# Weight rows of 8 KB, and turned tiles moved within SBUF in 16 pieces, in a two-layer encoder kernel

## The chip, the core and the metric

The kernel runs on one core of a Trainium2 chip, in one launch. The metric is device time in microseconds (us). The times before are 2138.24 us (median of three runs, 2136.27 to 2146.2). One further execution was profiled: it took 2142.62 us, and the span of its instructions is 2140.9 us. Every number of a profile is from that execution.

## What is computed

256 rows of 2048 floats go through two layers. All data are float32.

```python
# layer A                                       D = 2048, H = 16 heads of 128, FF = 8192
u = rms_norm(h, g);  q, k, v, fz = split(u @ a_w_in)          # (D, 3D + H)
q, k = rms_norm per head;  o = causal softmax attention with a forget bias
h = h + o @ a_w_out                                            # (D, D)
h = h + relu(rms_norm(h, g) @ mlp_w1[0]) ** 2 @ mlp_w2[0]      # (D, FF), (FF, D)
# shared keys and values, once, from h
k, v = split(rms_norm(h, g) @ kv_w)                            # (D, 2D)
# layer B
q = rms_norm(rms_norm(h, g) @ b_w_q);  o = chunked attention with a bias by distance
h = h + o @ b_w_out
h = h + relu(rms_norm(h, g) @ mlp_w1[1]) ** 2 @ mlp_w2[1]
```

## The kernel before

**Units.** Weights are consumed in units of 128 x 1024 floats, 512 KB each, 972 in all. For each unit, ScalarE (ACT) copies it, rounded, into `hi` and VectorE (DVE) writes the rest, `lo = raw - hi` (`issue`, L253 and L254). TensorE (PE) then makes three passes over it, hi by hi, hi by lo of the activations, and lo by hi (`passes`, L538, L540, L542). There are three `hi` and three `lo` buffers (pool `wsp`), and `fetch` keeps two units split ahead of the one being multiplied (`AHEAD`). A product unit is 12 matmuls (two k tiles, two row blocks, three passes).

**Pairs.** The two MLPs and the query projection use a Strassen-like scheme that needs seven block products where eight stand, on the first half of the k range of two neighbouring output panels. Such a `Pair` has seven forms, f0 to f6, each in two units of 6 matmuls, and eight product units a4 to a7 and b4 to b7. The forms' weights come from four blocks "11", "12", "21", "22" of 128 x 2048: `bring` (L276) loads a block into SBUF, `add` (L283) adds another block to it by an accumulating DMA of GpSimd (POOL), `make` (L290) adds two of them on DVE, and form 4 adds once more on DVE (L260). A chunk of an MLP is two pairs of w1 and two of w2; each MLP has four chunks.

**The written order.** `keep_order` fixes the order of every engine but POOL to that of the program text. `plan_mlp` deals the units of a stage by the strings in `ORDER` ("f0" is a form with both of its units, "a4" a product unit of the pair, "r" one left over from the pair before). `BEHIND` and `OPENING` say how many units after a form `bring`, `add` and `make` are written. Everything else (statistics, attention, the turning of tiles) is queued by `add_fill` and written one slot after each product unit or second form unit (`run_fill`). `HIDDEN`, `LONG` and `SHORT` hold, per output panel, the slots of the steps of a turned tile.

**Turned tiles.** A result of 256 x 512 has to be transposed before it can be an operand. DVE transposes its 32 x 32 blocks into `z`, 128 x 1024 (`blocks32`, L397). Then `carry` (from L408) brings the blocks to their partitions by way of HBM: `rows` writes `z` to a buffer `turn` in one DMA (L413), and `columns` reads it back in four DMAs of 32 partitions (L419). The four wait for the write. ACT uses the result in `take` (L896, the hidden layer), `split_turned` (L373, the normed residual) or `scale_q` (L662). `sums` (L355 to L364) then makes the form operands `Sh` and `S` of the first two panels: four DVE instructions, two ACT instructions on their result, two DVE instructions on that. 60 tiles are turned so, and 32 smaller ones in attention.

**Loading.** All DMAs but the accumulating ones are issued by SyncE (SP), in written order. `load` (L240) fetches one unit into one of six `raw` buffers; `fetch` keeps five loaded ahead (`EARLY`). In the built program every DMA of SP also waits for the eighth DMA that SP issued before it: eight are in flight at most.

Of the kernel before, what the change touches and what calls it, by code (L numbers as in the profile page):

```python
# [32 lines left out]
LONG = ((0, 0, 1, 3, 6, 7, 8, 8), (0, 0, 0, 1, 5, 5, 6, 6), (0, 0, 0, 0, 5, 6), (0, 0, 0, 2, 6, 6))  # L33
SHORT = ((3, 0, 1, 3, 5, 5, 7, 8), (6, 1, 2, 5, 10, 10, 14, 14), (3, 0, 3, 4, 8, 10), (0, 0, 0, 2, 5, 5))
REL = 384
ORDER = {
# [9 lines left out]
}  # L46
BEHIND = {
    (0, 0): [(0, 1, "make", 0)],
    (0, 1): [(0, 1, "make", 1), (1, 1, "add", "T1", 1)],
    (1, 0): [(3, 0, "bring", "12", 0)],  # L50
    (1, 1): [(2, 0, "bring", "12", 1)],
    (3, 0): [(2, 0, "bring", "11", 0)],
    (3, 1): [(2, 0, "bring", "11", 1)],
    (2, 0): [(1, 1, "add", "T1", 0)],
    (6, 1): [(5, 0, "add", "T3", 1)],
    (5, 0): [(2, 0, "add", "T3", 0)],
}
OPENING = (
    (20, "bring", "12", 0),
    (8, "bring", "12", 1),  # L60
    (8, "add", "T3", 0),
    (4, "add", "T3", 1),
    (7, "bring", "11", 0),
    (5, "bring", "11", 1),
# [17 lines left out]
def trunk(ctx: ExitStack, tc: tile.TileContext, xT, xr, gs, hg, bf, wgate, w_in, w_oa, f1a, s1a, f2a, s2a,  # L82
          w_kv, fqb, sqb, w_ob, f1b, s1b, f2b, s2b, rel, out):
# [9 lines left out]
    wraw = pool("wraw", 6)  # L93
# [42 lines left out]
    def queue(src, m):  # L136
        u = [src[i] for i in range(m)]
        n = KT // UA
        u[: 2 * n] = [u[i + q * n] for i in range(n) for q in range(2)]
        units.extend(u)  # L140
# [6 lines left out]
    class Tail:  # L147

        def __init__(self, src, first):
            self.left = [4]  # L150
            self.src = [[None] * (KT // UA - 4) + [src[first + u] for u in range(4)]]

    class Pair:

        def __init__(self, big, src, stage, n):
            self.big, self.src, self.stage, self.n = big, src, stage, n
            self.left = [6, 5]
            self.ps, self.t, self.done, self.prev, self.next = None, {}, set(), None, None

        def did(self, *names):  # L160
            return all((i, s) in self.done for i in names for s in range(2))

        def items(self, names):
            for i in names.split():
                if i[0] == "f":
                    for s in range(2):
# [4 lines left out]
    def pairs_of(f, s, c, stage):  # L171
        n = D // UN
        out = []
        for q in range(f.shape[0] // 4 // c[1]):
            i = c[0] * (f.shape[0] // 4 // c[1]) + q
            big = dict(zip(("11", "12", "21", "22"), (f[4 * i + j] for j in range(4))))
            src = [[None] * 4 + [s[8 * i + 4 * j + u] for u in range(4)] for j in range(2)]
            out.append(Pair(big, src, stage, q))
        return out

    def plan_mlp(w1, w2, wq, tail):
        pairs = []
        for c in range(NCH):
            pairs += pairs_of(*w1, (c, NCH), ("w1", c))
            pairs += pairs_of(*w2, (c, NCH), ("w2", c))
        if wq:
            pairs += pairs_of(*wq, (0, 1), ("q", 0))
        plan, rest = [], [Item(tail, 0, u) for u in range(KT // UA - 4, KT // UA)]
        for i, p in enumerate(pairs):
            own = list(p.items("a4 a5 a6 a7 b4 b5 b6 b7"))  # L190
            for j in ORDER["first" if not i else p.stage[0] + str(p.n) + ("+" if p.stage == ("w2", NCH - 1) else "")].split():
                if j == "r":
# [4 lines left out]
                else:  # L197
                    k = next(k for k in own if (k.kind, k.u) == ("ab".index(j[0]), int(j[1])))
# [5 lines left out]
        for p in pairs:  # L204
            g = lambda i, s=1: at[id(p), "f", i, s]
            assert g(0) < g(2, 0) and g(1) < g(2) < g(3, 0) and g(2) < g(5, 0) and g(3) < g(6, 0) and g(0) < g(4, 0)
            assert all(at[id(p), q, u, 0] > g((2, 3)[q]) for q in range(2) for u in range(4, 8))
# [5 lines left out]
    for i in range(w_in.shape[0]):  # L213
        units.append(w_in[i])
    n_out = w_oa.shape[0] - 4
    queue(w_oa, n_out)
    tail_a = Tail(w_oa, n_out)
    plan_a = plan_mlp((f1a, s1a), (f2a, s2a), (fqb, sqb), tail_a)
    for i in range(w_kv.shape[0]):
        units.append(w_kv[i])  # L220
    queue(w_ob, n_out)
    tail_b = Tail(w_ob, n_out)
    plan_b = plan_mlp((f1b, s1b), (f2b, s2b), None, tail_b)
# [4 lines left out]
    def load(parts=1):  # L228
        src, item = units.popleft(), None
        if isinstance(src, Item):  # L230
            item = src
            if item.u not in (4, 6):
                raws.append((item, None, ()))
                return
            src = item.pair.big[FORMS[item.u]][:, item.s * UN : (item.s + 1) * UN]
        raw = wraw.tile([P, UN], F32, name="raw")
        n = UN // parts
        cuts = [slice(i * n, (i + 1) * n) for i in range(parts)]
        for c in cuts:
            SY.dma_start(raw[:, c], src[:, c])  # L240
        raws.append((item, raw, cuts))

    def issue(parts=1):
        if not raws:
            load(parts)
        item, raw, cuts = raws.popleft()
        if not cuts:
            assert (FORMS[item.u], item.s) in item.pair.done
            raw, cuts = item.pair.t[FORMS[item.u]][:, item.s * UN : (item.s + 1) * UN], [slice(0, UN)]
# [6 lines left out]
        if item and item.u == 4:  # L256
            assert (2, item.s) in item.pair.done
            item.pair.done.add(("T4", item.s))
            t = item.pair.t["T4"] = item.pair.t["T2"]
            V.tensor_tensor(t[:, half(item.s)], t[:, half(item.s)], raw, op=ALU.add)  # L260
# [10 lines left out]
    def bring(p, name, s):  # L271
        assert not p.prev or p.prev.did(*((3,) if name == "11" else (1, "T2")))
        p.done.add((name, s))
# [4 lines left out]
    def add(p, name, s):  # L278
        to, block = {"T1": ("11", "12"), "T3": ("12", "22"), "T4": ("T2", "21")}[name]
        p.t[name] = p.t[to]  # L280
        assert (to, s) in p.done and (name == "T3" or {(0, s), ("T2", s)} <= p.done)
        p.done.add((name, s))
        G.dma_start(p.t[name][:, half(s)], p.big[block][:, half(s)], accum_op=ALU.add)  # L283
# [10 lines left out]
    def behind(p, i, s):  # L294
        for d, own, f, *a in BEHIND.get((i, s), ()):
            q = p if own else p.next
            if q is not None:
                while len(later) < d + 1:
                    later.append([])
# [789 lines left out]
```

## Time and profile before

| | us |
|---|---|
| median of the three runs | 2138.24 |
| the profiled execution, and its span | 2142.62, 2140.9 |
| TensorE busy in the span | 2087.9 (98%) |
| VectorE busy | 1733.5 (81%) |
| ScalarE busy | 1311.4 (61%) |
| bytes by DMA | 562.96 MB, 263 GB/s on average |

A row of a view names the line of the kernel, the engine, the operation and its tiles as out<-in, then how often it ran (x), its busy time and mean duration, and the idle time of its engine just before it with what ended that. PEld is the loading of the stationary operand, which runs beside PE. SPq is the DMA queue of SyncE. "PE acc L538 <- ACT hi L253" reads: a matmul of line 538 waited for the ACT instruction of line 253.

### The profile page before, as it was taken

The page shows a single profiled execution, that of the slowest core. Times are in us where ns is not written, and L with a number is a line of the kernel's source. Part 1 is how long each engine was busy: PE and PEld are TensorE (multiplying, and loading weights), DVE is VectorE, ACT ScalarE, POOL GpSimd, SP SyncE. Part 2 cuts the span into 40 slices and gives each one's busy share as a digit, 9 for nine tenths or more (in the row PEclk, how much of TensorE's full clock was granted, in tenths as well). Part 3 has the DMA queues.
Part 4 walks back from the last instruction along what each step waited for, and adds up shares of the span by engine and source line. Part 5 has one row for each costly group of instructions (what it writes and reads, how often), then busy time and mean ns, then how long its engine had stood idle before and what let it go on. Part 6 is the DMA issues. An engine that isn't in the chain of part 4 may idle for free. (4 is left out here: it accounts for less than half of the span.)

```text
span 2140.9 us, 26525 instructions
## 1 busy us (share of the span) xinstructions
PE 2087.9 (98%) x9114; PEld 1701.5 (79%) x9114; DVE 1733.5 (81%) x2003; ACT 1311.4 (61%) x1567; POOL 167.6 (8%) x184
## 2 busy tenths in 40 slices
PE   9999999999999999999999999999999999999999
PEld 7888888777877877887778888887778778778777
DVE  6767776888889888888989677678888897898887
ACT  6544545676567567566777545466765675675674
POOL 1101000000001000000002000000000000010000
PEclk9999999999999999999999999999999999999999
DMA  8787779999899899899987877798998998998995
GB/s 304 246 252 243 230 250 276 252 278 299 252 274 268 266 283 263 270 277 273 288 250 240 266 231 231 235 283 258 290 289 242 277 278 272 281 273 254 287 281 156
DMA packets 203479, 562.96 MB, mean 263 GB/s; under 512 B 39104, under 2 KB 76112, under 8 KB 203344
## 3 DMA queue, kind: packets, MB, share of 16 engines
q1 hardware_dynamic: 183760, 489.96, 68.8%
q0 software_dynamic: 19584, 71.31, 18.7%
q8 instruction: 71, 1.16, 0.2%
q14 instruction: 64, 0.52, 0.1%
HBM read 521.32 MB, written 39.87 MB: 262 GB/s over the span
## 5 line engine op out<-in xcount | busy, mean ns | idle before, releaser
L254 DVE TENSOR_TENSOR lo<-raw,hi 128x1024 fp32r<-128x1024 f32 (+1 forms) x634 | 759.0, 1214 | 236.8 <-ACT hi L253 222.8
L253 ACT ACTIVATE hi<-raw 128x1024 fp32r<-128x1024 f32 (+1 forms) x634 | 662.7, 1055 | 376.7 <-PE acc L540 218.2
L538 PE MATMUL acc<-hi,act 128*128 128x512 f32 x1644 | 462.4, 397 | 4.7 <-ACT hi L253 2.8
L540 PE MATMUL acc<-hi,act 128*128 128x512 f32 x1644 | 450.0, 390 | 0.0
L542 PE MATMUL acc<-lo,act 128*128 128x512 f32 x1644 | 448.8, 390 | 0.0
L538 PEld LDWEIGHTS acc<-hi,act 128*128 128x128 f32 x1644 | 306.7, 189 | 71.8 <-DVE acc L583 4.8
L540 PEld LDWEIGHTS acc<-hi,act 128*128 128x128 f32 x1644 | 309.0, 188 | 66.1 <-DVE act L343 1.0
L542 PEld LDWEIGHTS acc<-lo,act 128*128 128x128 f32 x1644 | 308.4, 188 | 65.1 <-DVE lo L254 0.6
L253 ACT ACTIVATE hi<-w 128x1024 fp32r<-128x1024 f32 x204 | 212.6, 1055 | 97.7 <-PE acc L540 35.9
L254 DVE TENSOR_TENSOR lo<-w,hi 128x1024 fp32r<-128x1024 f32 x204 | 245.1, 1215 | 24.8 <-ACT hi L253 24.7
L254 DVE TENSOR_TENSOR lo<-wT,hi 128x1024 fp32r<-128x1024 f32 x136 | 163.4, 1221 | 22.8 <-ACT hi L253 20.9
L253 ACT ACTIVATE hi<-wT 128x1024 fp32r<-128x1024 f32 x136 | 140.9, 1053 | 30.5 <-PE po L540 14.6
L538 PE MATMUL s<-hi,act 128*128 128x512 f32 x476 | 137.4, 393 | 9.8 <-ACT act L376 6.1
L542 PE MATMUL s<-lo,act 128*128 128x512 f32 x476 | 138.0, 395 | 2.1 <-DVE lo L254 1.9
L540 PE MATMUL s<-hi,act 128*128 128x512 f32 x476 | 137.6, 394 | 2.1 <-DVE act L377 2.0
L538 PEld LDWEIGHTS s<-hi,act 128*128 128x128 f32 x476 | 89.5, 189 | 30.9 <-ACT act L376 7.4
L542 PEld LDWEIGHTS s<-lo,act 128*128 128x128 f32 x476 | 89.1, 190 | 24.2 <-DVE lo L254 6.3
L540 PEld LDWEIGHTS s<-hi,act 128*128 128x128 f32 x476 | 90.2, 190 | 22.2 <-DVE act L377 3.4
L260 DVE TENSOR_TENSOR wT<-wT,raw 128x1024 f32<-128x1024 f32 x68 | 82.8, 1218 | 0.0
L290 DVE TENSOR_TENSOR wT<-w,w 128x1024 f32<-128x1024 f32 x68 | 82.8, 1218 | 0.0
L538 PE MATMUL po<-hi,act 128*128 128x512 f32 x272 | 73.0, 390 | 0.4 <-ACT hi L253 0.4
L540 PE MATMUL po<-hi,act 128*128 128x512 f32 x272 | 72.7, 389 | 0.0
(181 smaller groups left out, 2170.3 us busy)
## 6 DMA issues: line engine op xcount, KB each, us to landing
raw<-in_w_in SPq DMA_DIRECT2D x94, 512.0 KB, 4.6
raw<-in_s1a SPq DMA_DIRECT2D x64, 512.0 KB, 7.1
raw<-in_s2a SPq DMA_DIRECT2D x64, 512.0 KB, 7.3
raw<-in_w_kv SPq DMA_DIRECT2D x64, 512.0 KB, 4.8
raw<-in_s1b SPq DMA_DIRECT2D x64, 512.0 KB, 7.0
raw<-in_s2b SPq DMA_DIRECT2D x64, 512.0 KB, 7.1
turn<-z SPq DMA_DIRECT2D x60, 512.0 KB, 4.6
q<-turn SPq DMA_DIRECT2D x168, 128.0 KB, 6.6
```

The source lines that it names most:

```text
L253: S.activation(hi[:, c], raw[:, c], AF.Copy)
L254: V.tensor_tensor(lo[:, c], raw[:, c], hi[:, c].bitcast(F32), op=ALU.subtract)
L260: V.tensor_tensor(t[:, half(item.s)], t[:, half(item.s)], raw, op=ALU.add)
L290: V.tensor_tensor(p.t["T2"][:, half(s)], p.t["T3"][:, half(s)], p.t["11"][:, half(s)], op=ALU.add)
L538: TE.matmul(ps, xh, cut(hi, j), start=first, stop=False, **kw)
L540: TE.matmul(ps, xl, cut(hi, j), start=False, stop=False, **kw)
L542: TE.matmul(ps, xh, cut(lo, j), start=False, stop=last, **kw)
```

## The change

Four things change.

1. `load` fetches a block of 128 x 2048, 1 MB in rows of 8 KB, that serves two units (`Block`). There are three such buffers where there were six of half the size, and `fetch` keeps two blocks ahead (`EARLY = 2`) where it kept five units. The host lays the weights out to match. `bring` loads a whole block in one DMA; the accumulating DMAs stay at 128 x 1024.
2. 46 of the 60 turned tiles no longer pass through HBM. `moves` copies each 32 x 256 piece from `z` straight to its place in 16 DMAs, which are dealt in four groups of four to the slots of the tables. 14 tiles (the keys of both layers, the queries of layer A, two of the four query tiles of layer B) and the attention probabilities still use `carry`, with the read one slot behind the write.
3. `ORDER`, `BEHIND`, `OPENING`, `HIDDEN`, `LONG` and `SHORT` have new values, so units, loads and fill steps stand elsewhere.
4. At the start, the rows of `x` for the residual and their statistics are loaded and computed later.

PE, DVE, ACT and POOL execute the same instructions as before in another order (8974, 2005 and as many on the others). SP issues 1393 DMAs where it issued 1269.

```diff
-EARLY = 5
-HIDDEN = ((1, 4, 7, 7, 8, 8, 10, 12), (1, 3, 7, 8, 8, 8, 11, 11), (1, 2, 5, 6, 6, 9), (0, 1, 4, 7, 7, 8))
+EARLY = 2
+HIDDEN = (
+    (3, 3, 3, 3, 7, 7, 8, 10, 11, 11),
+    (0, 0, 0, 2, 7, 8, 8, 8, 10, 10),
+    (0, 2, 3, 4, 5, 5, 9, 9),
+    (0, 1, 2, 2, 4, 5, 8, 8),
+)
...
-    "w11": "f0 f1 r r f2 f4 a4 f3 a5 f5 f6 a6 a7 b4",
-    "w20": "r f0 r f1 f2 r f4 f3 f5 f6 a5 b4 a4 b5",
+    "w11": "r f0 f1 r f2 f4 a f3 a a f5 a f6 b b",
+    "w20": "r f0 r r f1 f2 f4 f3 f5 r a a r f6 b b",
...
-    wraw = pool("wraw", 6)
+    wraw = pool("wraw", 3)
...
+        new = block.raw is None
+        if new:
+            block.raw = wraw.tile([P, block.src.shape[1]], F32, name="raw", tag="raw")
+            if not parts:
+                SY.dma_start(block.raw, block.src)
...
     def bring(p, name, s):
...
         if not s:
             p.t[name] = qkv.tile([P, BIG], F32, name="w" + name, tag="Y" if name == "11" else "X", bufs=1)
-        SY.dma_start(p.t[name][:, half(s)], p.big[name][:, half(s)])
+            SY.dma_start(p.t[name][:, : p.subs * UN], p.big[name])
...
+    def moves(z, dst):
+        n = z.shape[1] // 4
+        d = dst.rearrange("p (i f) -> p i f", i=4)
+
+        def move(i):
+            for j in range(4):
+                SY.dma_start(d[32 * j : 32 * j + 32, i], z[32 * i : 32 * i + 32, j * n : (j + 1) * n])
+
+        return [lambda i=i: move(i) for i in range(4)]
...
-            way.extend(i[0] for i in carry(*zt, 0)[:2])
+            way.extend(moves(*zt))
...
-                    deal(HIDDEN[n], [i[0] for i in carry(*zt, 0)[:2]] + [step] * 6)
+                    deal(HIDDEN[n], moves(*zt) + [step] * 6)
```

More of the change, by code (lines that the diff above doesn't have):

```diff
@@ L197, in plan_mlp @@
                 else:
[L198 removed]
+                    k = next(k for k in own if k.kind == "ab".index(j))
                     own.remove(k)
@@ L256, in issue @@
         if item and item.u == 4:
[L257 to L260, printed above, removed]
+            add_on(item.pair, "T4", item.s, raw)
         if item:
@@ L304, in fetch @@
             issue()
-        while units and sum(1 for r in raws if r[2]) < early:
+        while units and sum(r[3] for r in raws) < early:
             load()
@@ L464, in f @@
                 step = steps(use)
-                do = [rows, turn, lambda: way[0](), lambda: way[1](), step, step, step, step]
-                deal(at[: 6 if fs is None else 8], do)
+                do = [rows, turn] + [lambda i=i: way[i]() for i in range(4)] + [step] * 4
+                deal(at[: 8 if fs is None else 10], do)
                 if then is not None:
@@ L647, in f @@
             if b == NB - 1:
-                turns = [[t] for _, _, _, t in rest] + carry(z, dst)
+                turns = [[t] for _, _, _, t in rest]
+                turns += carry(z, dst) if apart is None else [[m] for m in moves(z, dst)]
                 if apart is not None:
```

289 lines of the change are left out of this document (154 added, 135 removed), and 22 rows, old and new, of tables (LONG, ORDER, SHORT).

## The prediction

> **What bounds the kernel now.** I read the busy times first, then what matmuls waited for, then windows of the MLP, and the timeline where PE stood still.
>
> ```profile
> span 2140.9 us, 26525 instructions
> PE 2087.9 (98%) x9114; PEld 1701.5 (79%) x9114; DVE 1733.5 (81%) x2003; ACT 1311.4 (61%) x1567; POOL 167.6 (8%) x184
> ```
>
> PE is busy in all but 53 us of its span, and the change leaves it every matmul. A gain can come only from those 53 us and from matmuls that run slower than they can. This view names what matmuls waited for (total, times, longest):
>
> ```profile
> PE acc L538 <- ACT hi L253: 12.3, 10, 1.8
> PE po L542 <- DVE lo L254: 9.1, 8, 1.3
> PE s L538 <- ACT act L376: 6.1, 3, 2.4
> PE po L538 <- ACT hi L253: 5.0, 5, 1.6
> PE s L538 <- ACT hi L253: 3.7, 3, 1.6
> PE acc L542 <- DVE lo L254: 3.0, 9, 0.4
> PE s L540 <- DVE act L377: 2.0, 2, 1.4
> ```
>
> These seven are 41.2 us. All are waits for the splitting of weights or for operands made by ACT and DVE; none is a DMA. Windows tell where they lie (busy us and count of PE, PEld, DVE, ACT, POOL; granted clock; DMA share and GB/s):
>
> ```profile
> core 0: us, PE busy (x) PEld busy (x) DVE busy (x) ACT busy (x) POOL busy (x), PEclk, DMA share, GB/s
> 107.00:160.50 53.50, 53.50 (x244) 44.55 (x243) 35.81 (x52) 25.71 (x36) 2.70 (x2) 1.00 0.82 252
> 612.00:782.00 170.00, 165.96 (x715) 133.97 (x714) 144.31 (x144) 108.41 (x112) 13.81 (x16) 0.99 0.92 271
> 1850.00:2019.00 169.00, 165.22 (x720) 134.48 (x720) 145.78 (x146) 109.50 (x113) 13.65 (x16) 1.00 0.92 273
> 1070.00:1123.50 53.50, 49.17 (x204) 38.86 (x204) 47.13 (x52) 37.10 (x50) 3.44 (x4) 0.97 0.90 252
> ```
>
> The first is attention of layer A: PE never idles. The next two are about one MLP chunk each: 4.0 and 3.8 us idle, DVE at 85%, DMA at 92%. The last, around the query projection, idles 4.3 us in 53.5. So the time is PE's matmuls plus small stalls in the MLP stages, where DVE and DMA have little to spare. How short can a chunk be? From the chain of waits at the end, where nothing stalls:
>
> ```profile
> 2120.19 0.91 PE acc L538 x4
> 2131.07 0.91 PE acc L538 x4
> ```
>
> 48 matmuls start in these 10.88 us, 0.2267 us each. A product unit (12) takes 2.72 us and a form unit (6) 1.36 us; a pair has 8 and 14, 40.8 us, a chunk 163.2. The windows hold 169 to 170 us, about a chunk each: some 6 to 7 us of a chunk are lost, 4 as idle time and the rest in slow matmuls.
>
> **One stall in full,** from the timelines of the three engines:
>
> ```profile
> 622.60 0.42 DVE L355 TENSOR_TENSOR sum<-q 128x256 f32<-128x256 f32 x1
> 623.74 0.42 DVE L358 TENSOR_TENSOR sum<-q,sum 128x256 f32<-128x256 f32 x1
> 623.51 1.30 ACT L361 ACTIVATE Sh<-sum 128x512 fp32r<-128x512 f32 x2 [3.43 <-DVE sum L356]
> 624.72 3.88 ACT L253 ACTIVATE hi<-raw 128x1024 fp32r<-128x1024 f32 x4
> 625.81 0.73 PE L538 MATMUL acc<-hi,S 128*128 128x512 f32 x2 [1.83 <-ACT hi L253]
> 625.80:629.50 3.70, 3.69 (x10) 2.62 (x11) 3.70 (x4) 2.80 (x3) 0.00 (x0) 0.61 1.09 191
> ```
>
> DVE comes to the four sums at 622.60, ACT has stood 3.43 us waiting for them, rounds them (1.30 us), and only then makes the next `hi` (done about 625.8). PE had two form units, 2.72 us, in stock, and stands for 1.83 us. The last row is what follows: right behind the stall the granted clock is 0.61. [...]
>
> **The change part by part.** The sum is made against the profiled 2142.62 us (1.7 us lie outside the span); the median shown is 4.4 us lower, and I carry the difference over to it.
>
> *The new dealing.* How the stall row groups:
>
> ```profile
> L538 PE MATMUL acc<-hi,S 128*128 128x512 f32 x144 | 46.4, 404 | 9.5 <-ACT hi L253 9.5
> L542 PE MATMUL po<-lo,Sh 128*128 128x512 f32 x128 | 42.2, 411 | 9.5 <-DVE lo L254 9.1
> L361 ACT ACTIVATE Sh<-sum 128x512 fp32r<-128x512 f32 x32 | 20.2, 632 | 38.2 <-DVE sum L356 37.6
> ```
>
> The stall shown is one of six of its kind (chunks 2 to 4 of both MLPs). In the new order of DVE the sums of the first panel stand behind two product units and two form units; before, behind one product unit and two form units with an addition to `acc` between. Each product unit leaves DVE 2.72 - 1.22 = 1.5 us, so DVE reaches the sums some 1.5 us sooner, less what moved in front of them (`take`'s last step). I take 0.75 us of stall left where 1.6 stood: 9.5 - 6 x 0.75 = 5 us gained. The second kind (`po<-lo,Sh`) I leave: in both orders two additions of form 4 (L260), two transposes or an L583 addition and a `lo` meet within two form units. Bounds for the whole term: 0, and 18.6 us (9.5 + 9.1).
>
> *The clock.* The profile's 40 slices show 0.97 in seven, 53.5 x 0.03 = 1.6 us of lost matmul time each:
>
> ```profile
> 588.50:642.00 53.50, 51.48 (x217) 40.90 (x216) 45.19 (x47) 33.76 (x35) 4.30 (x5) 0.97 0.97 275
> 2033.00:2086.50 53.50, 52.23 (x221) 42.38 (x222) 47.06 (x49) 38.42 (x41) 4.25 (x5) 0.97 0.96 282
> ```
>
> About three of the seven follow the stall just shown; with 0.75 us they should not come: 5 us. Bounds 0 and 11.
>
> *The turns.* Who waited, and what a turn's transfers take:
>
> ```profile
> ACT q L896 <- DMA q<-turn: 50.5, 22, 5.7
> ACT y L373 <- DMA q<-turn: 9.3, 5, 3.0
> SPq L419 <- DMA turn<-z: 122.9, 41, 6.0
> L419 SPq DMA_DIRECT2D q<-turn x168: 325/430/1732, 344.1 to 2074.5; - x168
> DMA to landing us min/median/max: 2.9/6.6/12.4
> L413 SPq DMA_DIRECT2D turn<-z x60: 326/327/487, 56.0 to 2065.1; - x60
> DMA to landing us min/median/max: 1.9/4.3/10.4
> ```
>
> (The first landing row is of the reads into `q`, the second of the writes.) From `z` to the operand: 4.3 (write lands) + 4 x 0.43 (SP issues the reads) + 6.6 = 12.6 us, and SP stands 122.9 us in all before the reads. After: 16 issues and one landing. The trace has no 32-partition copy within SBUF. An issue lies between 0.327 and 0.43 us, so 16 take 5.2 to 6.9; the landing between 2.9 and 6.6. Together 8.1 to 13.5, which is 4.5 us sooner to 0.9 later; I take the middle, 1.8 sooner, since one hop replaces two. The tables allow about what they did: for the first hidden panel four slots from the last move to `take` (three before, from the reads), for the third one slot (three before), so that one may come later. PE's share of turn lateness is in `s<-hi,act` behind L376 and L377 and partly L253 (6.1 + 2.0 + 3.7 us) with about three of the slow slices (5 us): I take half, 8 us. Bounds: 17 gained, or the loss of the first rival.
>
> *8 KB rows and HBM.* Removed are 46 x 2 passes of 512 KB through HBM (a write and a read), added 46 within SBUF: 24 MB of 562.96 less, some 4% of the DMA share, and about half of the weight packets.
>
> ```profile
> q1 hardware_dynamic: 183760, 489.96, 68.8%
> HBM read 521.32 MB, written 39.87 MB: 262 GB/s over the span
> ```
>
> No matmul waited for a DMA, so this alone is worth nothing on the path, 0; what it hides behind is the two units split ahead. What a packet of 8 KB takes no row shows; between half and the whole of two of 4 KB, either way no cost here.
>
> *Fewer, larger buffers.* The stock falls from five units to two blocks, at least three units when the next block is issued: 3 x 2.72 = 8.2 us in a run of product units, plus the two units split ahead.
>
> ```profile
> DMA to landing us min/median/max: 3.2/6.2/11.4
> ACT hi L253 <- DMA raw<-in_w_in: 7.8, 9, 2.6
> ```
>
> A 512 KB load lands in 6.2 us (median); a block in 6.2 to 12.4. That is mostly within 8.2 + 5.4. I take 1 us lost at the start, where ACT already waits for loads, and 1 us elsewhere; bounds 0 and the first rival. The later loads of `x` rows have no reader in the first panel: 0.
>
> *SP.* 736 moves x 0.327 to 0.43 = 241 to 316 us replace 46 x (0.327 + 4 x 0.43) = 94 of issuing and about as much of waiting; 382 blocks replace 764 loads, 125 us less. SP stays under half of the span. POOL's accumulating DMAs are as many; behind them stands nothing that PE is near.
>
> Sum: -5 - 5 - 8 + 2 = -16 for the profiled execution; 2138.2 - 16 gives 2122 us.
>
> **The rivals.** *SP's bursts (slower).* Most moves stand 12 or 16 in a row, and a ninth transfer waits for the first of the eight before it. A burst then takes 5.2 to 6.9 us of issuing plus a landing in its middle (2.9 to 6.6): 8 to 13 us in which no weight load is issued. The next block lands 6.2 to 12.4 us later, 14 to 26 us after the last one, against 4 x 2.72 + 2.72 = 13.6 us of stock (two blocks and what is split). It decides from the point where that landing passes 13.6 us. At 0.9 us per turned tile, 46 x 0.9 = 41 us less the 16: 2163 us; at 0.5 us, 2145. For it: the SP rows, DMA at 92%. Against it: form units in between stretch the stock, and SP already stands 123 us for the reads today. [...]
>
> *The stalls only move (no change).* DVE is at 85% of a chunk whatever the order, so removed collisions come back at other slots, and the moves of the third panel are late by what the first gains: 41 us of waits stay, 2138 us.
>
> *The DMA was behind it all (much faster).* If most lateness came from slow landings, chunks go down to 166 us: 8 x 4 = 32 us, with five slow slices (8 us) about 2098 us. Against it: the stall shown has no DMA in it.
>
> That 8 KB rows do nothing (are cut into packets of 4 KB) would change none of these.
>
> **How the numbers follow.** Forecast 2122: 0.50; much faster: 0.08; no change: 0.16; bursts: 0.26. 0.5% (about what a measurement can tell) is 10.7 us. Faster (below 2127.5): 0.50 + 0.08 = 0.58; the same 0.16; slower 0.26. The forecast's own range is 2104 (turn and dealing terms near their upper bounds) to 2136. For 8 in 10 it has to hold most of the bursts too: 2102 to 2163, which leaves out about half of the fast case and half of the slow one.
>
> **What would show it.** Right: PE idle near 40 us in the span; the wait of `acc<-hi,S` for L253 below 6 us; four or fewer slices at 0.97; ACT's wait for `q<-z` (L949 in the new code) under 40 us; HBM written near 16 MB. Wrong: `hi` (ACT) waiting for `raw` by tens of us, PE idle above 60 us, or moves landing 8 us and more after their issue, which would be the bursts. Unchanged waits of `acc<-hi,S` would undo the first two terms.

## The result: 0.7% slower, and the profile after

| | before | changed |
|---|---|---|
| median, us | 2139.64 (5 runs) | 2157.19 (5 runs) |
| ratio, 95% interval | | 1.0072 (1.0045 to 1.0098) |
| profiled execution, span | 2142.62, 2140.9 | 2157.28, 2155.5 |
| TensorE idle in the span | 53.0 us | 62.0 us |

The forecast was 2122 us, faster. The page of the changed kernel, first the span, the busy times and the bytes of HBM, then what matmuls waited for (total, times, longest):

```profile
span 2155.5 us, 26474 instructions
PE 2093.5 (97%) x9114; PEld 1701.9 (79%) x9114; DVE 1735.8 (81%) x2003; ACT 1306.0 (61%) x1567; POOL 166.6 (8%) x184
...
HBM read 497.20 MB, written 15.75 MB: 238 GB/s over the span
```

```profile
PE po L776 <- DMA pbuf<-turn: 12.3, 5, 3.3
PE po L587 <- DVE s L632: 11.3, 9, 2.5
PE acc L587 <- ACT hi L287: 9.8, 6, 2.8
PE acc L587 <- DVE acc L632: 4.4, 8, 0.6
PE s L587 <- ACT hi L287: 4.1, 3, 2.2
```

The lines have moved: L287 makes `hi`, L288 `lo`, L587 is the first of the three passes, L949 the first step of `take`, L412 that of `split_turned`, L451 the moves, L776 the product of probabilities and values. The first row is new: matmuls wait for the transposed attention probabilities (`pbuf`), which go over HBM as before. In the MLPs both stalls that the prediction showed are gone, and another has grown (4.6 us before, for `hi`):

```profile
L587 PE MATMUL acc<-hi,S 128*128 128x512 f32 x144 | 44.3, 389 | 0.0
L591 PE MATMUL po<-lo,Sh 128*128 128x512 f32 x128 | 41.6, 406 | 0.5
L587 PE MATMUL po<-hi,Sh 128*128 128x512 f32 x128 | 40.9, 400 | 9.2 <-DVE s L632 8.8 <-ACT hi L287 0.3
```

Of the 9.2 us 8.8 are eight waits of 1.10 us, one in each chunk, for an addition by DVE (L632). The windows say where the time went (columns as in the prediction). First the two MLP chunks shown of before, then the ends of attention in layers A and B, then the place between the query projection and the keys:

```profile
612.00:782.00 170.00, 167.75 (x732) 136.39 (x731) 148.16 (x146) 110.61 (x116) 13.92 (x16) 1.00 0.86 263
1850.00:2019.00 169.00, 166.91 (x729) 135.71 (x728) 147.64 (x146) 108.56 (x113) 13.76 (x16) 1.00 0.87 265
321.00:374.50 53.50, 46.12 (x184) 36.80 (x183) 26.24 (x35) 21.16 (x29) 0.00 (x0) 0.90 0.62 191
1391.00:1444.50 53.50, 45.65 (x188) 36.18 (x188) 26.40 (x39) 18.96 (x29) 1.80 (x2) 0.94 0.56 171
1123.50:1177.00 53.50, 48.02 (x197) 38.03 (x198) 47.75 (x60) 37.83 (x51) 12.06 (x9) 0.95 0.59 203
```

The last three in the trace before:

```profile
321.00:374.50 53.50, 53.26 (x239) 43.94 (x237) 35.65 (x43) 30.51 (x46) 1.73 (x2) 1.00 0.92 276
1391.00:1444.50 53.50, 53.12 (x236) 43.53 (x235) 38.56 (x45) 32.26 (x48) 2.56 (x3) 1.00 0.95 284
1123.50:1177.00 53.50, 53.46 (x236) 43.83 (x235) 51.94 (x67) 40.11 (x54) 13.57 (x9) 1.00 0.74 236
```

The chunks did get faster: 732 and 729 matmuls start where 715 and 720 did, about 4 and 2 us. The last three windows idle 7.4, 7.9 and 5.5 us where they idled 0.2, 0.4 and 0.0, at clocks of 0.90 to 0.95, with the DMA at 56 to 62%, where it stood at 74 to 95% before: it was not bandwidth that ran short. (The work between query and keys idled before too, 4.3 us in the window ahead of this one, which the prediction shows; counted by matmuls 4200 to 5000, PE waited 9.2 us before and 15.2 after.) The moves themselves (times of an issue in ns, minimum, median and maximum, and of the landing in us):

```profile
L451 SPq DMA_DIRECT2D q<-z x672: 507/589/2139, 350.9 to 2085.1; - x168
DMA to landing us min/median/max: 1.7/4.1/7.9
```

An issue takes 0.589 us (median), not 0.327 to 0.43. The first tile of the output projection, from the timeline of layer A:

```profile
350.88 10.10 SPq L451 DMA_DIRECT2D q<-z  x16
361.09 1.07 PE L587 MATMUL acc<-hi,act 128*128 128x512 f32 x4
362.34 1.71 ACT L412 ACTIVATE y<-q,gsb 128x256 f32<-128x256 f32 x4 [6.34 <-DMA q<-z]
364.09 1.06 ACT L415 ACTIVATE act<-y 128x1024 fp32r<-128x1024 f32 x1
365.05 1.04 ACT L287 ACTIVATE hi<-raw 128x1024 fp32r<-128x1024 f32 x1
366.14 2.08 PE L587 MATMUL acc<-hi,act 128*128 128x512 f32 x4 [2.17 <-ACT hi L287]
```

SP issues for 10.10 us. ACT, which works in written order, has stood 6.34 us for the tile when the last piece lands; the next `hi` is written behind that, and PE, out of split units, stands 2.17 us. Then its four matmuls take 2.08 us where four took 1.07: half speed, at a granted clock of 0.52 from 366 to 369 us. No weights are missing here.

The start of the n-th matmul, against before's, places this in the whole program (each column is one execution, which may lie some 10 us off its kernel's median, as e7's does; e1 to e15 are the experiments):

```
matmul, up to            after    e5    e4    e2    e7   e10    e14
1400 attention A           2.5   1.1   1.1   1.7   3.3   0.2    0.4
1600 first turn behind it 14.9   6.8   1.8   4.8   9.1   0.2    4.9
1800 output projection A  15.2   7.1   5.0   5.0   9.3  -1.1    5.1
4200 most of MLP A         0.2  -4.2 -11.4 -13.9 -10.2 -16.7   21.3
5000 query, first keys     9.0   6.0  -2.6  -9.8  -1.9 -14.4   48.1
5800 most of attention B   9.0   6.0  -2.6  -9.8  -1.9 -14.4   48.1
6200 first turn behind it 25.9  12.4   2.8  -7.4  10.3 -13.3   54.2
9000 MLP B                14.9   2.7  -6.9 -24.7  -6.4 -26.8   85.7
```

In the first trace after, 11 us are won from matmul 6200 to the end and 15 from 1800 to 4200, and more than that is lost at the hand-offs between stages.

### The profile page after: what moved, and what is told of

It reads as the page before. It is cut to its first block, busy times and chain, and to the rows that moved or that the text cites. A ratio compares the mean times of both kernels' runs of the same rounds, so it can differ in the third digit from the quotient of the medians.

```text
span 2155.5 us, 26474 instructions
## 1 busy us (share of the span) xinstructions
PE 2093.5 (97%) x9114; PEld 1701.9 (79%) x9114; DVE 1735.8 (81%) x2003; ACT 1306.0 (61%) x1567; POOL 166.6 (8%) x184
## 2 busy tenths in 40 slices
DMA packets 150678, 538.85 MB, mean 250 GB/s; under 512 B 41088, under 2 KB 78096, under 8 KB 101648
## 3 DMA queue, kind: packets, MB, share of 16 engines
HBM read 497.20 MB, written 15.75 MB: 238 GB/s over the span
## 4 chain that ended last, share of the span: by engine, by line
PE 81%; DVE 6%; DMA 5%; SPq 3%; ACT 3%; issue 2%; DVEq 0%; ACTq 0%; POOLq 0%
PE acc L587 17%; PE acc L589 17%; PE acc L591 17%; PE po L591 5%; PE po L587 5%; PE po L589 5%; PE s L589 4%; PE s L591 4%; PE s L587 4%; DVE lo L288 3%; SPq L451 3%; ACT hi L287 1%; DMA q<-z 1%; DMA pbuf<-turn 1%; DMA turn<-pbuf 1%
## 5 line engine op out<-in xcount | busy, mean ns | idle before, releaser
L288 DVE TENSOR_TENSOR lo<-raw,hi 128x1024 fp32r<-128x1024 f32 (+1 forms) x634 | 759.3, 1214 | 206.0 <-ACT hi L287 202.7
L287 ACT ACTIVATE hi<-raw 128x1024 fp32r<-128x1024 f32 (+1 forms) x634 | 658.5, 1053 | 365.7 <-PE acc L589 199.0
L587 PE MATMUL acc<-hi,act 128*128 128x512 f32 x1644 | 468.3, 401 | 18.9 <-ACT hi L287 9.8
L587 PEld LDWEIGHTS acc<-hi,act 128*128 128x128 f32 x1644 | 308.4, 190 | 89.7 <-ACT hi L287 13.5
L287 ACT ACTIVATE hi<-w 128x1024 fp32r<-128x1024 f32 x204 | 214.6, 1056 | 104.4 <-PE po L589 52.0
L288 DVE TENSOR_TENSOR lo<-w,hi 128x1024 fp32r<-128x1024 f32 x204 | 245.5, 1221 | 34.5 <-ACT hi L287 32.7
L287 ACT ACTIVATE hi<-wT 128x1024 fp32r<-128x1024 f32 x136 | 142.3, 1057 | 65.0 <-PE po L589 24.9
L288 DVE TENSOR_TENSOR lo<-wT,hi 128x1024 fp32r<-128x1024 f32 x136 | 162.7, 1221 | 20.9 <-ACT hi L287 20.3
L587 PE MATMUL s<-hi,act 128*128 128x512 f32 x476 | 136.4, 391 | 6.5 <-ACT hi L287 4.1
L587 PEld LDWEIGHTS s<-hi,act 128*128 128x128 f32 x476 | 89.2, 188 | 27.2 <-ACT hi L287 5.3
L591 PEld LDWEIGHTS s<-lo,act 128*128 128x128 f32 x476 | 88.3, 189 | 28.2 <-DVE lo L288 10.8
L779 ACT ACTIVATE act<-po 128x256 fp32r<-128x256 f32 x32 | 12.3, 385 | 102.1 <-PE po L777 102.1
L587 PE MATMUL po<-hi,act 128*128 128x512 f32 x272 | 73.1, 391 | 0.0
```

The lines of the kernel that those rows point to most:

```text
L287: S.activation(hi[:, c], raw[:, c], AF.Copy)
L288: V.tensor_tensor(lo[:, c], raw[:, c], hi[:, c].bitcast(F32), op=ALU.subtract)
L587: TE.matmul(ps, xh, cut(hi, j), start=first, stop=False, **kw)
L591: TE.matmul(ps, xh, cut(lo, j), start=False, stop=last, **kw)
L779: S.activation(o[i][:, 0], po[:, :T], AF.Copy)
```

## The experiments

Every ratio is to runs of the kernel before on the same chip, with its 95% interval.

**e5: the changed kernel again.**

> The changed kernel once more, unaltered, for a second trace and as a measure on the chip of the next runs. It tells which of its stalls are the kernel's own and which one execution's. Theory: the gaps behind the first burst of the two output projections (2.1 to 3.2 us) and the three between the query projection and the keys (1.69, 1.56, 2.32 us) come again to 0.1 us; PE's waits for the probabilities (12.3 us over 5 in the first trace) vary, between 2 and 12 us. Rival: those waits are 12 us again, so they belong to the changed order. The time is 0.5 to 1.0% above before's.

2151.03 against 2137.93 us: 1.0062 (1.0037 to 1.0086). The wait for the probabilities was 2.8 us (2 times) instead of 12.3: it belongs to the execution as much as to the kernel. The gap behind the first burst came again, 2.56 us between matmul starts both times in layer A and 3.23 and 3.40 in layer B.

**e1: all tiles by way of HBM; e4: those of the output projections alone.** `both` gives the two steps of `carry`, the write and the read. e4 has the table `SHORT` of before. e1 has the new tables with two slots, for the write and the read, where the moves had four (3 and 4 for the first hidden panel).

```diff
-            way.extend(moves(*zt))
+            way.extend(both(*zt))
...
-SHORT = (
-    (5, 0, 0, 0, 0, 0, 3, 3, 5, 7),
-    (7, 0, 0, 1, 2, 5, 9, 10, 13, 13),
...
+SHORT = ((3, 0, 1, 3, 5, 5, 7, 8), (6, 1, 2, 5, 10, 10, 14, 14), (3, 0, 3, 4, 8, 10), (0, 0, 0, 2, 5, 5))
```

> The changed kernel, with every turned tile by way of HBM again (2 slots of each table for the write and the read in place of 4 for the moves); dealing of units, 1 MB loads and start as changed. Theory (the moves' issue, 0.59 us each on SP, costs at the first turn of each output projection and takes SP from the attention's transfers; the gain of the MLPs is the dealing's): the two PE gaps behind the first burst (2.1 and 3.2 us) go, ACT's wait in the output projection (about 7 us) falls to 3, the MLPs keep their gain of 24 us, about 2142 (2135 to 2149). Rival A (the MLPs' gain is the moves'): the MLP stalls come back, 2165 to 2180. Rival B (the moves are immaterial, the 1 MB loads are what costs): 2153 to 2161, the gaps in front of the output projections stay.

> The changed kernel, with the residual's turned tiles of the two output projections alone by way of HBM, with the table that these stages had before; all else as changed. Theory (first burst too late for its reader): PE's gaps of 2.1 and 3.2 us at the second panel go with the slow clock behind them, about 2147 (2140 to 2152). Rival A (what is lost there is lost at the end of attention, before the first move): 2153 to 2159, the gaps stay or move on by a few us. Rival B (a burst is cheaper than two hops in these stages too): slower than 2159.

e1: 2148.35 against 2135.7, 1.007 (1.0045 to 1.0095), as slow as the changed kernel: the theory's 2142, forecast for a before of 2138, missed, and by its time this is rival B. Its MLPs win 9.7 and 8.7 us where the first trace after won 15 and 11, and the gap behind the first burst of layer B stayed (3.52 us), since ACT waits up to 7.3 us there for the tile over HBM as well. e4: 2138.42, 1.0016 (1.0000 to 1.0032): 0.5% better than the changed kernel, and the gaps at matmuls 1576 and 6100 are gone. So the tiles of these two short stages, their way and their table together, are worth 10 to 12 us; which of the two does it was not run apart.

**e2: four DMAs a tile.**

```diff
-            for j in range(4):
-                SY.dma_start(d[32 * j : 32 * j + 32, i], z[32 * i : 32 * i + 32, j * n : (j + 1) * n])
+            SY.dma_start(d[:, i], z[:, i * n : (i + 1) * n])
```

> The changed kernel, with each turned tile moved by 4 DMAs of 128 partitions instead of 16 of 32 partitions. The blocks then stay in their own partitions, so that part of the transposition is left out of the computation. Bytes and tables as changed. Theory (the price is 16 issues): a tile costs SP 4 x 0.5 = 2 us instead of 10.1, the gaps behind the first burst go, about 2144 (2136 to 2150). Rival A (the tile's landing counts, or the moves only collide with loads, by their bytes): no change, 2153 to 2161. Rival B (the 1 MB loads are what costs): at most 4 us gained.

This kernel leaves out the part of the transposition that takes blocks to other partitions, so it prices the issues and does not compute the whole result. 2118.0 against 2135.7: 0.9921 (0.99 to 0.9943), far below the 2144 of the theory. The same bytes, a quarter of the issues:

```profile
L450 SPq DMA_DIRECT2D q<-z x168: 464/593/1564, 344.8 to 2035.5; - x168
DMA to landing us min/median/max: 1.9/5.3/9.0
```

A piece of 128 partitions costs the same 0.59 us of SP as one of 32, and lands 1.2 us later. No ACT instruction waits for a move any more. ACT's `hi` waits for weights (the rows of `raw` added up) 77 us in this trace, 79 after and 15 before: what the forecast had called the sign of the bursts is there at full size in the faster kernel too, so by itself it costs nothing.

**e6, e7, e12: other queues for the pieces.** Shown is e7, SP and POOL; e6 has `(SY, S)`, SP and ACT, and e12 `G` alone.

```diff
-                SY.dma_start(d[32 * j : 32 * j + 32, i], z[32 * i : 32 * i + 32, j * n : (j + 1) * n])
+                (SY, G)[j % 2].dma_start(d[32 * j : 32 * j + 32, i], z[32 * i : 32 * i + 32, j * n : (j + 1) * n])
```

> The changed kernel, with half of the 16 pieces of every moved tile issued by ACT's DMA queue and half by SP's; tables, dealing, loads and pieces as changed. Theory (SP's 16 issues of 0.59 us in a row are the price): SP needs 4.7 us for a tile, the gaps behind the first bursts shrink below 1 us; ACT pays up to 8 x 0.59 = 4.7 us a tile but has 39% to spare: 10 to 25 us faster than the changed kernel, 0.5 to 0.0% below before's time. Rival (an issue stops ACT as it does SP, and ACT's hi comes late): PE's waits for ACT's hi rise above 30 us, slower than the changed kernel by 10 us and more.

> The changed kernel, with half of the 16 pieces of every moved tile issued by POOL's DMA queue and half by SP's. Theory (issues on SP are the price): 8 issues on SP take 4.7 us; POOL, 8% busy, issues 512 KB in 0.94 us, 8 pieces in at most 7.5 us beside it: 8 to 20 us faster than the changed kernel. Rival (POOL's pieces stand behind its accumulating transfers, which wait for ACT and DVE): ACT's waits for q from z rise above 60 us, and the time is the changed kernel's or above.

> As e7_pool_half, with all 16 pieces of every moved tile issued by POOL. Theory (only SP's share of the issues costs, as long as a tile is there in time): a tile takes 16 x 0.50 = 8.0 us on POOL instead of 4.7, so the first bursts of the output projections come late again (a gap of about 1 us each) and POOL's accumulating transfers wait for them; SP is free: within 6 us of e7, 2121 to 2133 against a before of 2138. Rival A (SP's issues still cost in e7): 2115 or less. Rival B (the accumulating transfers come late behind the pieces, and f1 and f2 wait): above 2145.

e7: 2126.43 against 2137.93, 0.9956 (0.9938 to 0.9975), 1.1% below the changed kernel on the same chip (25 us, where the theory said 8 to 20): the first version that beats both. POOL issues a piece in 0.503 us, and ACT's waits for tiles are down to 3.8 us (`y`) and nothing in `take`. e6: 2300.65, 1.0773 (1.0745 to 1.0801), the rival's outcome, far beyond its 10 us. ACT's issues, and the wait behind them:

```profile
L451 ACTq DMA_DIRECT2D q<-z x336: 514/601/2035, 344.5 to 2222.5; - x168
```

```profile
ACT hi L287 <- DMA q<-z: 146.6, 25, 9.4
```

ACT's own work now waits behind the pieces that it issues; its 39% of spare time is of no use, as the spare time does not lie at that place of its order. e12: 2185.31 against 2137.04, 1.0211 (1.0191 to 1.0231), the time of rival B but hardly its mechanism: ACT's `hi` waits only 6 us for blocks of the forms. SP issues no piece at all, and yet `take` waits for tiles (POOL's issues, then ACT's waits):

```profile
L451 POOL DMA_DIRECT2D q<-z x672: 496/501/856, 343.2 to 2111.2; - x168
```

```profile
ACT q L949 <- DMA q<-z: 53.2, 16, 9.5
```

So SP's time is not the whole price; it counts when the sixteenth piece lands. 16 x 0.50 = 8.0 us on one queue came out worse than the 9.4 on SP. The likely reason, argued and not tested, is that the pieces stand behind accumulating transfers in POOL's order, which waited for DVE for up to 26.6 us. e7 moves as many bytes as the changed kernel (538.89 and 538.85 MB), so its 25 us come from the queues that issue the pieces.

**e9, e10: the moves alone in the kernel before** (44 tiles; order, loads of 512 KB and start as before), from SP and from SP and POOL.

```diff
...
+    def spread(at, k):
+        a, b = at[k], at[k + 1]
+        return at[:k] + tuple(a + (b - a) * i // 3 for i in range(4)) + at[k + 2 :]
...
-                    deal(HIDDEN[n], [i[0] for i in carry(*zt, 0)[:2]] + [step] * 6)
+                    deal(spread(HIDDEN[n], 0), moves(*zt) + [step] * 6)
```

> The kernel before, with one part of the change alone: 44 turned tiles (hidden panels and residual) go by 16 moves each, dealt evenly over the slots from the write to the read of the tables before; the two query tiles stay with HBM. Dealing of units, loads of 512 KB and start as before. Theory (16 issues of 0.59 us on SP are dear, and dearer where SP also issues 764 loads): 704 x 0.59 = 415 us of SP in bursts of 9.4 us; 0.5 to 1 us lost per tile, 2157 to 2180 against 2138. Rival (the prediction's: the moves are worth 8 us, what is lost comes with the dealing and the larger loads): 2125 to 2136.

> As e9_moves_alone, with half of the pieces issued by POOL's queue. Theory (the dealing and the 1 MB loads are worth some 18 us in the MLPs, the moves with two queues another 8): faster than e9 by 15 us and more, but above e7_pool_half (2126 against a before of 2138) by 5 to 20 us: 2131 to 2146. Rival (the dealing is worth nothing once the moves are cheap): within 4 us of e7, 2122 to 2130.

e9: 2195.62 against 2137.04, 1.0263 (1.0241 to 1.0285). e10: 2114.95, 0.989 (0.9874 to 0.9907), the fastest of all, below what its theory and its rival gave. The wait of `take` (L915 here) in e9, then the two of `take` in e10, then the page of e10, in which PE idles 39.6 us:

```profile
ACT q L915 <- DMA q<-z: 72.5, 18, 7.7
```

```profile
ACT q L915 <- DMA raw<-in_s2b: 15.3, 4, 4.6
ACT q L915 <- DMA raw<-in_s2a: 14.3, 4, 4.0
```

```profile
span 2113.8 us, 27601 instructions
PE 2074.2 (98%) x9114; PEld 1695.5 (80%) x9114; DVE 1732.4 (82%) x2003; ACT 1311.6 (62%) x1567; POOL 345.4 (16%) x536
```

In e10 the trace puts the waits of `take` down to loads of weights, which `take` does not read. In each of these eight a piece of a moved tile had landed 0.26 to 0.41 us before `take` began, so they may be waits for the tile all the same.

**e3, e8, e14, e13: smaller loads.** e3 and e8 load the 8 KB buffers by halves, e14 and e13 (shown) undo the 1 MB loads wholly, with `EARLY = 5`.

```diff
-    wraw = pool("wraw", 3)
+    wraw = pool("wraw", 6)
...
+        raw = wraw.tile([P, UN], F32, name="raw", tag="raw")
+        for c in cuts:
+            SY.dma_start(raw[:, c], block.src[:, half(s)][:, c])
```

> The changed kernel, with each block loaded by two DMAs of 512 KB (rows of 4 KB) at two places of the written order, five units ahead as before, into the same three 8 KB buffers; the forms' blocks still come whole; dealing and moves as changed. Theory (1 MB loads hold up the transfers of the attention's probabilities and make ACT wait for raw): PE's waits for the probabilities (12.3 us over 5) go below 4, ACT's waits of hi for raw fall from 75 us by half, about 2145 (2137 to 2150). Rival A (the probabilities are late because the read stands right behind the write on SP, whatever the size of a load): those waits stay above 9, 2153 to 2161. Rival B (bursts alone): at most 3 us gained.

> As e3_halves_all, but with four units loaded ahead instead of five. In e3 the fifth unit ahead needed a fourth 8 KB buffer whenever the unit at hand was a block's second half, so SP stood in front of a load until that unit was split, and everything behind it on SP stood too. Theory (that was the loss of e3, and loads by halves are otherwise no better or worse than whole blocks): within 6 us of the changed kernel, PE's waits for ACT's hi back from 97 us to below 30. Rival A (1 MB loads hold up other transfers): 8 us and more faster than the changed kernel. Rival B (twice as many load issues on SP, 0.33 us each, or 4 KB rows cost): 15 us and more slower than the changed kernel.

> The changed kernel (16 moves on SP) with the 1 MB loads undone alone, as in e13. Theory (1 MB loads are what makes the moves bearable: 382 issues less on SP): near e9_moves_alone, 2175 to 2200. Rival (the new dealing and its tables do that): near the changed kernel, 2140 to 2158.

> As e7_pool_half, with the 1 MB loads undone alone: each unit of 512 KB (rows of 4 KB) is loaded by itself into one of six buffers, five ahead, as before the change; the forms' blocks still come whole; dealing and moves as in e7. Theory (1 MB loads hold up the probabilities' transfers, the dealing holds up the query projection): PE's waits for the probabilities go below 2 us, the gaps of 1.69, 1.56 and 2.32 us between query and keys stay: 5 to 9 us faster than e7, about 2120 against a before of 2138. Rival A (the dealing makes the probabilities late): as e7, 2123 to 2130. Rival B (382 more issues on SP cost more than that): slower than e7 by 5 us and more.

e3: 2275.07, 1.0654 (1.0626 to 1.0681): five units ahead do not fit three buffers, and this run tells only what a blocked SP costs. e8, with four: 2188.8, 1.0243 (1.0215 to 1.0272), its rival B; whether the number of issues or the 4 KB rows cost this, the run does not tell. e14: 2223.57, 1.0401 (1.0377 to 1.0424). The theory that 1 MB loads hurt falls: without them the changed kernel is 3.4% slower than with them (e5). e14 has a stall of 7 us in each of the eight chunks; the first, with the same place of the changed kernel (matmul 2094) below it:

```profile
472.81 7.14 SPq L445 DMA_DIRECT2D q<-z  x8
480.05 0.53 SPq L268 DMA_DIRECT2D raw<-in_f2a  x1
480.62 2.63 SPq L445 DMA_DIRECT2D q<-z  x4
483.75 0.67 SPq L300 DMA_DIRECT2D w<-in_f2a  x1
484.97 2.41 SPq L445 DMA_DIRECT2D q<-z  x4
489.24 1.06 ACT L943 ACTIVATE q<-q 128x1024 f32<-128x1024 f32 x1 [7.69 <-DMA q<-z]
492.38 1.22 PE L581 MATMUL po<-hi,Sh 128*128 128x512 f32 x2 [6.96 <-ACT hi L281]
```

```profile
476.33 9.45 SPq L451 DMA_DIRECT2D q<-z  x12
487.35 1.06 ACT L949 ACTIVATE q<-q 128x1024 f32<-128x1024 f32 x1 [0.53 <-DMA q<-z]
490.59 0.66 PE L587 MATMUL po<-hi,Sh 128*128 128x512 f32 x2
```

In both, `take` is the instruction in front of the `hi` that PE needs. In e14 ACT stands there 7.69 us and PE 6.96; in the changed kernel the last piece comes 0.53 us late, and PE doesn't notice. In e14 the pieces stand among loads in SP's order. e13, the same with two queues, has ACT wait again, and the probabilities no more:

```profile
ACT q L943 <- DMA q<-z: 32.7, 12, 4.7
```

```profile
PE po L770 <- DMA pbuf<-turn: 1.7, 2, 1.6
```

Yet it is 2136.15, 0.9989 (0.9975 to 1.0002): slower than e7 by 0.3%, or 7 us: rival B. The first half of its theory held, the sum didn't.

**e11: the probabilities by POOL's queue, on top of e7; e15: another order of the query's second panel, on top of e7.**

```diff
-        st["carry"] = carry(z, st["pT"])
+        st["carry"] = carry(z, st["pT"], G)
...
-    "q1": "f0 f1 f2 f4 r r a f5 r r a f3 b b f6",
+    "q1": "f0 f1 f2 f4 r r r r a f5 a f3 b b f6",
```

> As e7_pool_half, and the write and the four reads of the attention's probabilities are issued by POOL's queue too. Theory (their write stands behind 1 MB loads in SP's queue, 8 us at the longest, and so PE waits 3 to 12 us for them): PE's waits for the probabilities go below 2 us, SP's 124 us in front of the reads go, 3 to 10 us faster than e7: about 2120 against a before of 2138. Rival (POOL's transfers take longer, or stand behind its powers for the softmax's and norms' rows): those waits stay or grow, no faster than e7.

> As e7_pool_half, with another order of the query projection's second panel alone: the four units left over from the first panel stand together behind f4 (f0 f1 f2 f4 r r r r a f5 a f3 b b f6), so the first panel ends two units earlier and the steps that it starts (the flipped operands for the keys) stand two slots earlier. Theory (these steps are what ACT and DVE come late with in the keys' first panel): the gaps of 1.56 and 2.32 us go, 3 to 5 us faster than e7. Rival (the second panel ends too late, whatever the first does): the gap of 1.69 us at the first matmul of the keys and the two others stay, within 2 us of e7.

e11: 2124.86 against 2137.04, 0.9932 (0.9914 to 0.9949), not to be told from e7; PE's waits for the probabilities were 8.9 us (2 times, 6.4 the longest), so the theory missed. e15: 2128.6 against 2138.14, 0.9963 (0.9948 to 0.9977), within 2 us of e7 as its rival had it; new gaps of up to 2.99 us stand where the old ones were.

**Put together,** by way of the tiles and by order and load size (ratio to before):

| | order before, 512 KB | new order, 512 KB | new order, 1 MB |
|---|---|---|---|
| over HBM | 1 | not run | 1.007 (e1) |
| 16 pieces on SP | 1.0263 (e9) | 1.0401 (e14) | 1.0072, 1.0062 (the change) |
| 8 on SP, 8 on POOL | 0.989 (e10) | 0.9989 (e13) | 0.9956 (e7) |
| 4 of 128 partitions | not run | not run | 0.9921 (e2) |
| 16 on POOL | not run | not run | 1.0211 (e12) |
| 8 on SP, 8 on ACT | not run | not run | 1.0773 (e6) |

The column "new order" holds the tables, the start and the whole loads of `bring` too. The old order with 1 MB loads was not tried: it does not use the two units of a block near each other, as three buffers ask for.

## Why the prediction was wrong

*The turns (the step that failed).* The prediction put "An issue lies between 0.327 and 0.43 us, so 16 take 5.2 to 6.9", and "Together 8.1 to 13.5", from which it took the middle, 10.8 us, 1.8 sooner than over HBM, worth 8 us. The rows it went by were loads and reads that have HBM at one end (of these it left out `nb<-cd`, four reads of 0.62 us). A copy within SBUF costs 0.589: 16 x 0.589 = 9.4 us of SP, and 10.10 in the burst shown. Counted in the traces from its first issue to its last landing, each of the 42 tiles that come as `q` took 11.4 to 17.8 us, median 14.7, beyond the range. Over HBM it had taken 15.7, not the 12.6 that the medians of the rows add up to, since slots of the tables lie between write and reads. So by this count the tile came 1.0 us sooner, where 1.8 was forecast; what the sum did not have is a burst that holds SP for 10 us and a tile that stays beyond the range.

e7 is the test of this step: with 8 pieces on each of two queues a tile takes 11.2 us, about the 10.8 of the forecast, and the change is 9 us faster than before where it was 13 to 15 slower. How the pieces are issued is thus some 23 of the 29 to 31 us between forecast and result; e2, where a tile takes 8.9 us, agrees. Within a column of the table above the median time of a tile goes with the time of the kernel (14.7, 15.7 and 17.4 us for e10, before and e9), but not across: e10's tiles take as long as the changed kernel's. On SP the moves alone cost 2.6% (e9), from two queues they win 1.1% (e10). The idea behind the term was right, and its size above 8 us: e10 won 22 us. Against tiles over HBM in the new order the moves on SP won nothing (e1); but e1's tiles take 17.4 us, later than before's, so it does not price the rest of the change by itself.

*The places between the stages were put at nothing.* This is the second step that failed, and it is in e7 too, which wins 9 us and not 16. The sum has terms for the MLPs, the turns and the loads, and none for what the new order does where one stage ends and the next begins. In the MLPs (matmuls 1800 to 4200 and from 6200) the first trace after won 26 us, and PE's waits there fell from 35 to 19 us. From 4200 to 5000 every kernel of the new order lost time; in the trace after, single waits there are 2.6 us for an addition by DVE (L632), 1.8 for `lo` and 1.9 for `qn`. At the ends of attention the probabilities came late, by 2.8 to 12.3 us in sum.

*Fewer, larger buffers: +2 was forecast.* The sign is wrong. Undone, they cost 3.4% with the moves on SP (e14 against e5) and 0.3% with two queues (e13 against e7). A 1 MB block is issued in 0.328 us, as a 512 KB unit is, so the change saves 382 issues and as many places at which SP waits for a buffer with pieces behind it. The block lands in 6.3 us (median) where a unit took 6.2, the near end of the forecast's "6.2 to 12.4". That the saved issues are the gain is argued: the rows of 8 KB and the stock of buffers change with them, and no run parts the three. What they may cost is the probabilities: PE waited for them 2.8 to 12.3 us in the traces with 1 MB loads, 0 to 1.9 in those without (6.6 in e3). That the write to HBM stands behind a block is argued, not shown; e11 did not confirm it.

*The new dealing: -5 was forecast.* In the MLPs it did more: the waits of `acc<-hi,S`, `po<-lo,Sh` and `po<-hi,Sh`, 9.5 + 9.5 + 4.6 us before, are 0.0 + 0.5 + 9.2, 14 us less, and the second kind, which the prediction left, went with the first. But part of it came back at other slots, as the rival "The stalls only move" had it: all of the 9.2 but 0.4 are the waits for DVE's additions, and `acc` waits another 4.4 us for them (1.4 before). And the dealing doesn't carry the kernel. With 512 KB loads and two queues the whole new order is slower than the old by 1.0% (e13 against e10), with the moves on SP by 1.3% (e14 against e9). PE idles 51.1 us in e13 and 39.6 in e10, and its waits for DVE's additions are 16.5 us against 2.5. That is a part of the loss; which of the tables makes it, or the pieces that stand closer together in them than in e10, is open. By matmul index e13 loses against e10 4 us from 1800 to 4200, 5 from 4200 to 5000 and 4 from 6200 to 9000 (e13 stands at 1.4, -10.2, -3.1, -1.6 and -10.8 at these five). The loss between query and keys (4200 to 5000) is 4 us and more in every kernel with the new order against 2 in e10, though e9 loses 11 there too; e15 did not find its cause.

*The clock: -5 was forecast.* It rose to 1.00 in the MLP windows, as forecast, and fell elsewhere: 53.5 x (0.10 + 0.06 + 0.05) = 11 us at the three hand-offs. Over all 40 slices the lost matmul time was about 12 us before and 17 after. The stall of 2.17 us had half speed behind it (a granted clock of 0.52 from 366 to 369 us), and so had that of 1.83 us before (0.50 from 627.5 to 629.5 us), but length alone does not decide: behind a stall of 2.55 us at 1088 us of the same trace the clock stayed at 1.00 (1088 to 1092 us). So, in these traces, taking stalls of this size away gives no fixed gain of clock.

*The tables "allow about what they did".* Not at the output projections, where the last piece is issued 10 us after the first and the reader stands three slots (8.2 us) behind: the 10 to 12 us of e4.

*The rivals.* The bursts, put at 2145 to 2163, came true in time (2157) and in place (no weight load is issued in 10 us), not in mechanism: the prediction had the next block of weights come late. ACT does wait 79 us for weights, and e2, which waits 77, is faster than before. What comes late is the tile; ACT stands in front of it in `take` or `split_turned`, and `hi` is late behind ACT. ACT's waits for DMAs in these two (L949 and L412, or the same lines elsewhere; those that the trace books to weights are counted in, 34 of e10's 37 us) rank most kernels of each column as their times do: old order 37 us (e10), 64 (before), 116 (e9); new order with 512 KB 44 (e13), 107 (e14); with 1 MB 0 (e2), 4 (e7), 35 (e4), 42 (e5), 56 (e1), 77 (e12). e6 is the exception: ACT issues pieces itself there, and it is `hi` that waits (146.6 us). Across columns they don't: before waits more than the change and is faster, and e10 waits as long as e4, which is 1.3% slower. Of the signs, HBM written (15.75 MB), `acc<-hi,S` below 6 us and `take`'s wait under 40 (26.3) came as for the forecast; PE idle above 60 and seven slices below a clock of 1.00, where four were to be, came as against it. The first three measure what the change did, not what it cost.

## What to carry to other kernels

Price an issue by a row of the same kind of transfer (which memories at its ends), and if there is none, take the worst row, times the number of pieces: the worst here, 0.62 us (`nb<-cd`), times 16 gives 9.9 us, and the burst shown took 10.10. A tile that is cut into 16 pieces is there when the sixteenth has landed. Look at which instruction waits for it in an engine that works in written order, and what stands behind that instruction; the wait costs there (ACT stood 6.34 us for the tile shown, and PE 2.17 us for the `hi` behind it). Pieces can go to a second queue whose engine has nothing urgent behind them (POOL here, 0.9956 in e7, not ACT, 1.0773 in e6), and with the moves on SP loads of twice the size paid: 382 issues fewer, and without them the kernel is 3.4% slower (e14 against e5).

## Of the hardware

- Issue time went with the kind of transfer more than with its size (medians): 0.33 us on SP for a load of 512 KB (before) or 1 MB (the trace after) of weights from HBM over 128 partitions, 0.43 for a read of 32 partitions of a turned tile from HBM (before), 0.59 for a copy of 32 KB over 32 partitions within SBUF (after). A copy of 128 KB over 128 partitions took 0.59 into `q` and 0.47 into `land` (e2). The same 32 KB piece into `q` took 0.50 us on POOL (e7) and 0.60 on ACT (e6).
- A load of 1 MB in rows of 8 KB landed in 6.3 us (median, the trace after), one of 512 KB in rows of 4 KB in 6.2 (before).
- Of stalls of TensorE of about 2 us some had half the clock behind them and some had not: 2.17 us at 366 us (0.50 in the 2 us behind it), 2.55 us at 1088 us (1.00 in the 4 us behind it), both in the trace after.
- Issues held up ACT's own work: with half of the pieces on its queue instead of POOL's, the kernel took 174 us more (e6 against e7), 3.8 us for each of 46 tiles, though ACT was busy for 57% of the span (e6).
- Moving the same bytes in four times as many DMAs cost 30 us (1.0062 against 0.9921 of 2138, e5 and e2, whose pieces stay in their partitions). Issuing a tile takes SP 4 x 0.593 = 2.4 us in e2 and 16 x 0.589 = 9.4 us in e5, though a piece of e2 lands later, in 5.3 us (median) against 4.1 in e5.
